# Group-weight products of a pooling branch: from one fp32 matmul to three matmuls of split operands

## The chip, the core and the metric

The kernel computes one decoder layer on one core of a Trainium2 chip. The metric is device time in microseconds (us) for one execution; less is better. Before the change it is 623.25 us, the median of three runs (622.22 to 624.1).

## What is computed

The layer takes `x` (512 tokens, 1024 channels, float32) and runs two token mixers side by side, attention and a causal pool, merges them through gates, and adds a gated MLP. The change is in the pool:

```python
proj = h @ w_in                      # q | k | v | p | gate logits
for g, w in enumerate((2, 4, 8, 16)):            # four groups of 128 channels of p
    pooled = (causal trailing mean of p over w tokens)
    diff = pooled - p
y = einsum('bsgc,gcd->bsgd', diff, w_group) * scale    # per group: 512x128 times 128x128
y_pool = y @ w_branch_pool
```

So the products in question are four, one for each group: a 128x128 weight against a 128x512 difference.

## The kernel before

Nearly all products are taken in float32r with operands cut in two. A helper `split(hi, lo, src)` (lines 72 to 78) lets ACT copy `src` into `hi` (rounded to float32r, L76) and DVE subtract `hi` from `src` into `lo` (L77). A helper `mm3` (lines 249 to 255) then issues three matmuls into one accumulator: `whi*ahi` (L251), `whi*alo` (L254), `wlo*ahi` (L255). The four group products were the exception: `pool_out(j)` took one matmul of plain float32 operands (L485), and ACT copied the result to `zT`, times the scale (L486).

**Input projections.** Two of the pooling tiles (groups 3 and 2) are plain products of 8 x 3 matmuls of 512 columns (tiles named `p`). All others are taken in pairs by a Strassen-like scheme of seven products instead of eight, `seven()` (lines 293 to 319): pair 0 is pooling groups 0 and 1, pairs 1 to 4 are the query and key tiles. Each pair needs four weight tiles, named after their product: A (a plain load), X (a sum of two loads), Y (computed on DVE from A and X, L211) and D (a half-width load). Each is split into `whi` and `wlo` before use. The banks of a pair are `sai`, `sbi`, `sci`. X of pair 1 is summed on DVE (L204). For pairs 0, 2, 3 and 4, X is loaded in two steps: SP issues a plain load into `xr` (L192), and GpSimd (POOL) issues a second DMA that adds another part of the weight onto it (L194, below called the accumulate). X of pair 2 is below called X2, and so on. A product of a pair can't begin before its tile is loaded and split.

**Pooling.** `pool_sum(j)` copies a projected tile from the accumulator to a buffer `pt` (ACT, L460), and adds shifted copies of it, log2(w) times, into buffers `pw` (L465): for group 3 on DVE, for the others on POOL. `pool_dif(j)` turns the last of them into the difference, in three DVE operations (L477, L478, L480). All these buffers come from one ring, tag `tmp`, of seven (`TMP = 7`): the eighth buffer that is drawn reuses the first, and its first writer waits for the first one's last reader. In program order group 3 draws `pt3` and four `pw`, group 2 `pt2` and three, group 0 `pt0` and one, group 1 `pt1` and two.

**What sets the order.** The source is recorded in program order; a scheduler then reorders it by its own estimate of times and writes one in-order queue for each engine. An instruction that waits holds back all that stands behind it on its engine. POOL's queue holds the pooling adds, the accumulates (L194) and the attention's bias-strip loads (L387), all in one row.

After the projections come the attention scores of the first head pair (L559; banks `sc`). `first_scores()` (line 607) takes the group products of groups 0 and 1 just before them.

Of the kernel before, what the change touches and what calls it, by code (L numbers as in the profile page):

```python
# [9 lines left out]
F32R = mybir.dt.float32r  # L10
# [4 lines left out]
P = 128  # L15
S = 512
# [14 lines left out]
PAD = 16  # L31
# [4 lines left out]
TMP = 7  # L36
# [16 lines left out]
def layer_kernel(ctx: ExitStack, tc: tile.TileContext, xT, x, w_v, w_c, rel_bias, invcnt, w_group,  # L53
                 pscale, w_br, w_out, lnr, w_fi, convp, w_fo, out):
    nc = tc.nc
# [9 lines left out]
    def bank(name):  # L65
        return ps.tile([P, S], F32, tag="ps", name=name)
# [5 lines left out]
    def split(hi, lo, src, copy=None):  # L72
        if copy:
            copy(hi, src)
        else:
            state["hi"] = nc.scalar.activation(hi, src, AF.Copy)  # L76
        state["lo"] = nc.vector.tensor_tensor(lo, src, hi.bitcast(F32), op=ALU.subtract)  # L77
        return state["lo"]
# [170 lines left out]
    def mm3(out_, w, a, start, stop, pin=False, **kw):  # L249
        (wh, wl), (ah, al) = w, a  # L250
        ins = nc.tensor.matmul(out_, wh, ah, start=start, stop=False, **kw)  # L251
        if pin:
            tc.keep_in_program_order(ins)
        nc.tensor.matmul(out_, wh, al, start=False, stop=False, **kw)  # L254
        state["mm"] = nc.tensor.matmul(out_, wl, ah, start=False, stop=stop, **kw)  # L255
# [80 lines left out]
    pb = pooling.enter_context(tc.tile_pool(name="pb", bufs=1, side="right", reuse_waits="tile"))  # L336
    wg = pb.tile([P, 4, P], F32, name="wg")
# [10 lines left out]
    for i in range(WARM):  # L348
        nc.tensor.matmul(wb_, *(nc.const_aps.tensor(1.0, [P, n], mybir.dt.bfloat16) for n in (P, S)),
                         start=True, stop=True)  # L350
# [89 lines left out]
    dif = {}  # L440
# [28 lines left out]
    def pool_dif(j, *behind):  # L469
        w = POOL_WINDOWS[j]  # L470
        pt, cur = sums.pop(j)
        with ExitStack() as held:
            for ins in behind:
                held.enter_context(tc.issue_after(ins.ins))

            d, x_ = cur[:, PAD:], pt[:, PAD:]
            nc.vector.tensor_tensor(d[:, :w - 1], d[:, :w - 1], cinv[:, :w - 1], op=ALU.mult)  # L477
            nc.vector.scalar_tensor_tensor(d[:, w - 1:], d[:, w - 1:], 1.0 / w, x_[:, w - 1:], op0=ALU.mult,  # L478
                                           op1=ALU.subtract)
            nc.vector.tensor_tensor(d[:, :w - 1], d[:, :w - 1], x_[:, :w - 1], op=ALU.subtract)  # L480
            dif[j] = d

    def pool_out(j):
        b = bank(f"zb{j}")
        nc.tensor.matmul(b, wg[:, j, :], dif[j], start=True, stop=True)  # L485
        nc.scalar.activation(zT[:, j, :], b, AF.Copy, scale=psc[:, j:j + 1])  # L486

    def in_tile(kind, j):
# [118 lines left out]
    def first_scores():  # L607
        nonlocal aw, standing
        pool_out(0)
        pool_out(1)  # L610
        pooling.close()
        aw = attn.enter_context(tc.tile_pool(name="aw", bufs=4, side="right", reuse_waits="tile"))
        standing = scores(0, True)
        next(standing)

    aw = standing = None
    for n in range(1 + pairs):
        if n == 0:
            u, done = xr[1][:, 3, :], lambda ba, u: pool_sum(0, ba)
        else:  # L620
            u = raw_k[n - 1] = qraw[n - 1][:, S:]
            done = lambda ba, u, p=n - 1: heads_done(p, ba)
        seven(("i", n), (xT_hi, xT_lo), ti, own(n), u, done, first_scores if n == 3 else None, begun.get(n))
        if n == 0:
            behind_sum.close()
            pool_dif(PLAIN[0], state["Y"])
            pool_sum(PLAIN[1], second)
            with tc.issue_after(state["acc"].ins):
                write_table(table)
        elif n == 1:  # L630
            pool_out(PLAIN[0])
            pool_dif(PLAIN[1], state["add"])
            pool_dif(0, state["add"])
            pool_sum(1, xr[1][:, 3, :], -1.0)
            add1 = state["add"]
        elif n == 2:
            pool_out(PLAIN[1])
            pool_dif(1, add1)
            with tc.issue_after(state["acc"].ins):
                load_strip(0)  # L640
                load_strip(1)
            split_heads(0, state["add"], state["copy"])
        elif n == 3:
            begin(pairs)
            list(standing)
            split_heads(1)
# [45 lines left out]
    def br_mm(f, br, b=None, ks=range(4), pin=False):  # L692
        key, o = (("br", f), 4 * br) if f >= 6 else (("oz"[br], f // 2), f % 2 * 4)
        wh, wl = split3(weights(at[key]), KT)
        b = b or bank(f"br{f}_{br}")
        for k in ks:
            src = (zT_hi[:, k, :], zT_lo[:, k, :]) if br else (oT_hi[:, k, :], oT_lo[:, k, :])
            mm3(b, (wh[:, o + k, :], wl[:, o + k, :]), src, k == 0, k == 3, pin and k == ks[0])
        return b
# [97 lines left out]
    for n, (f, br) in enumerate(order):  # L797
# [4 lines left out]
        b = br_mm(f, br)  # L802
# [17 lines left out]
    def gate_done(f, ba, u):  # L820
        if f < KT - 1:
            for br, v, scale in ((0, ba, 1.0), (1, u, -1.0)):
                nc.scalar.activation(v, v, AF.Sigmoid, scale=scale)
                nc.vector.tensor_tensor(branch[f, br], branch[f, br], v, op=ALU.mult)
            merged(f, branch[f, 0], branch[f, 1])
            unused.append(branch[f, 1])
        else:
            for br, v, scale in ((0, ba, 1.0), (1, u, -1.0)):
                gslot[8 * br + f] = unused.pop(0)
                nc.scalar.activation(gslot[8 * br + f], v, AF.Sigmoid, scale=scale)  # L830
# [6 lines left out]
    for f in range(GSEVEN, KT):  # L837
        if f == KT - 1:
# [3 lines left out]
              lambda ba, u, f=f: gate_done(f, ba, u), first_half if f == KT - 1 else None)  # L842
# [443 lines left out]
```

## Time and profile before

| | |
|---|---|
| median of three runs | 623.25 us (622.22 to 624.1) |
| the profiled execution's own time | 622.81 us |
| its span in the trace | 621.1 us |
| TensorE (PE) busy | 612.5 us, 99% of the span |
| VectorE (DVE) busy | 511.3 us, 82% |
| ScalarE (ACT) busy | 355.8 us, 57% |
| GpSimd (POOL) busy | 115.6 us, 19% |
| group products (L485) | 4 products in 8 records, from 49.8 to 73.5 us |

The trace is one execution. A row of the timeline gives start and duration in us, the engine, the line of the kernel, the operation, and out<-in by the program's tile names without their buffer numbers; a bracket at the end gives idle time ahead of it and what ended that. Matmuls are pipelined, so the start of one to the start of the next is what it costs PE, not its duration. A float32 matmul shows as two records.

### The profile page before, as it was taken

The page shows a single profiled execution, that of the slowest core. Times are in us where ns is not written, and L with a number is a line of the kernel's source. Part 1 is how long each engine was busy: PE and PEld are TensorE (multiplying, and loading weights), DVE is VectorE, ACT ScalarE, POOL GpSimd, SP SyncE. Part 2 cuts the span into 40 slices and gives each one's busy share as a digit, 9 for nine tenths or more (in the row PEclk, how much of TensorE's full clock was granted, in tenths as well). Part 3 has the DMA queues.
Part 4 walks back from the last instruction along what each step waited for, and adds up shares of the span by engine and source line. Part 5 has one row for each costly group of instructions (what it writes and reads, how often), then busy time and mean ns, then how long its engine had stood idle before and what let it go on. Part 6 is the DMA issues. An engine that isn't in the chain of part 4 may idle for free.

```text
span 621.1 us, 10681 instructions
## 1 busy us (share of the span) xinstructions
PE 612.5 (99%) x4129; PEld 553.1 (89%) x4129; DVE 511.3 (82%) x793; ACT 355.8 (57%) x541; POOL 115.6 (19%) x133
## 2 busy tenths in 40 slices
PE   9999999999999999999999999999999999999995
PEld 6899998777899998889999999999999888888884
DVE  5888876868778888399999888898988869798886
ACT  6736668557556567134676565666666355555452
POOL 0033207351212101110120010101100302123301
PEclk9999999999999999999999999999999999999998
DMA  8567544029966324807685567677635997889805
GB/s 319 196 204 199 173 147 125 35 77 298 216 173 181 75 96 143 335 5 252 128 245 124 148 180 194 182 195 202 194 84 166 330 250 146 205 189 200 209 1 135
DMA packets 41042, 107.98 MB, mean 174 GB/s; under 512 B 4240, under 2 KB 4760, under 8 KB 40736
## 3 DMA queue, kind: packets, MB, share of 16 engines
q1 hardware_dynamic: 26944, 70.72, 32.9%
q0 software_dynamic: 13472, 35.67, 29.2%
q10 hardware_dynamic: 576, 0.92, 0.4%
q8 instruction: 32, 0.52, 0.3%
q14 instruction: 18, 0.15, 0.1%
HBM read 105.18 MB, written 3.17 MB: 174 GB/s over the span
## 4 chain that ended last, share of the span: by engine, by line
PE 98%; DVE 1%; DMA 1%; DVEq 0%; issue 0%
PE saf L251 5%; PE saf L255 5%; PE saf L254 5%; PE v L435 3%; PE fi L251 3%; PE fi L255 3%; PE fi L254 3%; PE sbf L251 3%; PE sbf L254 3%; PE sbf L255 3%; PE br L251 2%; PE br L255 2%; PE br L254 2%; PE wo L251 2%; PE wo L255 2%; PE wo L254 2%
## 5 line engine op out<-in xcount | busy, mean ns | idle before, releaser
L77 DVE TENSOR_TENSOR wlo<-araw,whi 128x1024 fp32r<-128x1024 f32 x58 | 71.9, 1247 | 9.8 <-ACT whi L76 9.2
L76 ACT ACTIVATE whi<-araw 128x1024 fp32r<-128x1024 f32 x58 | 60.8, 1058 | 30.0 <-PE saf L254 6.2
L77 DVE TENSOR_TENSOR wlo<-wraw,whi 128x1024 fp32r<-128x1024 f32 (+1 forms) x47 | 55.8, 1195 | 14.9 <-ACT whi L76 14.6
L76 ACT ACTIVATE whi<-wraw 128x1024 fp32r<-128x1024 f32 (+1 forms) x47 | 47.4, 1019 | 30.2 <-DMA wraw<-in_w_fo 8.4
L76 ACT ACTIVATE whi<-tw 128x1024 fp32r<-128x1024 f32 (+1 forms) x30 | 29.5, 984 | 23.6 <-DMA tw<-in_w_fo 9.1
L77 DVE TENSOR_TENSOR wlo<-tw,whi 128x1024 fp32r<-128x1024 f32 (+1 forms) x30 | 33.5, 1130 | 6.7 <-ACT whi L76 6.7
L251 PE MATMUL saf<-hT_hi,whi 128*128 128x256 f32 x136 | 37.9, 279 | 0.0
L251 PE MATMUL sbf<-T_hi,whi 128*128 128x256 f32 x136 | 37.9, 279 | 0.0
L251 PE MATMUL saf<-nT_hi,whi 128*128 128x256 f32 x136 | 37.8, 278 | 0.0
L254 PE MATMUL saf<-hT_lo,whi 128*128 128x256 f32 x136 | 37.8, 278 | 0.0
L255 PE MATMUL saf<-nT_hi,wlo 128*128 128x256 f32 x136 | 37.8, 278 | 0.0
L254 PE MATMUL sbf<-T_lo,whi 128*128 128x256 f32 x136 | 37.7, 278 | 0.0
L255 PE MATMUL sbf<-T_hi,wlo 128*128 128x256 f32 x136 | 37.7, 278 | 0.0
L254 PE MATMUL saf<-nT_lo,whi 128*128 128x256 f32 x136 | 37.7, 277 | 0.0
L255 PE MATMUL saf<-hT_hi,wlo 128*128 128x256 f32 x136 | 37.7, 278 | 0.0
L194 POOL DMA_DIRECT2D xraw<-in_w_fi x13 | 15.7, 1205 | 116.2 <-DMA xraw<-in_w_fi 62.7
L254 PE MATMUL fi<-hT_lo,whi 128*128 128x256 f32 (+1 forms) x112 | 36.2, 326 | 0.0
L255 PE MATMUL fi<-hT_hi,wlo 128*128 128x256 f32 (+1 forms) x112 | 36.2, 326 | 0.0
L251 PE MATMUL fi<-hT_hi,whi 128*128 128x256 f32 (+1 forms) x112 | 36.1, 327 | 0.0
L239 POOL DMA_DIRECT2D tw<-in_w_fo x18 | 15.6, 902 | 59.8 <-DVE wlo L77 59.8
L595 POOL TENSOR_SCALAR pp<-pp,rs 128x128 f32<-128x128 f32 (+3 forms) x32 | 21.1, 680 | 25.0 <-DVE rs L592 25.0
L254 PEld LDWEIGHTS saf<-hT_lo,whi 128*128 128x128 f32 x136 | 25.5, 188 | 0.0
(359 smaller groups left out, 2208.9 us busy)
## 6 DMA issues: line engine op xcount, KB each, us to landing
tw<-in_w_fo POOLq DMA_DIRECT2D x20, 512.0 KB, 7.4
araw<-in_w_fi SPq DMA_DIRECT2D x17, 512.0 KB, 3.8
xraw<-in_w_fi SPq DMA_DIRECT2D x13, 512.0 KB, 3.9
xraw<-in_w_fi POOLq DMA_DIRECT2D x13, 512.0 KB, 6.6
araw<-in_w_c SPq DMA_DIRECT2D x12, 512.0 KB, 4.6
wraw<-in_w_fi SPq DMA_DIRECT2D x10, 512.0 KB, 3.7
wraw<-in_w_fo SPq DMA_DIRECT2D x10, 512.0 KB, 5.5
tw<-in_w_fo SPq DMA_DIRECT2D x10, 512.0 KB, 6.9
```

The costliest lines, as they stand in the source:

```text
L76: state["hi"] = nc.scalar.activation(hi, src, AF.Copy)
L77: state["lo"] = nc.vector.tensor_tensor(lo, src, hi.bitcast(F32), op=ALU.subtract)
L194: state["acc"] = nc.gpsimd.dma_start(v, bass.AP(tensor=a.tensor, offset=a.offset, ap=[[pst, pn], [u.offset + S - a.offset, 2], [est, S]]), ...
L239: nc.gpsimd.dma_start(raw, half(then[1:], sl), accum_op=ALU.add)
L251: ins = nc.tensor.matmul(out_, wh, ah, start=start, stop=False, **kw)
L254: nc.tensor.matmul(out_, wh, al, start=False, stop=False, **kw)
L255: state["mm"] = nc.tensor.matmul(out_, wl, ah, start=False, stop=stop, **kw)
L435: ins = nc.tensor.matmul(bs[j], xs_[j][a], (wh, wl)[b], start=kt == 0 and n == 0, stop=False)
L595: state["norm"] = nc.gpsimd.tensor_scalar(pp[:, offs[i]:offs[i] + n], pp[:, offs[i]:offs[i] + n], rs[:, i:i + 1], 1.0, op0=ALU.mult, op1=A ...
```

## The change

The group weight `wg` is split once, when the first difference is formed. Each difference is split into two new buffers, `hi` and `lo`, which are drawn from the same ring of seven as the sums. The product becomes `mm3`.

```diff
@@ pool_dif / pool_out
-            dif[j] = d
+            if not dif:
+                split(*wgs, wg)
+            dif[j] = tuple(pb.tile([P, PAD + S], F32R, tag="tmp", name=f"dif{j}_{q}", bufs=TMP)[:, PAD:]
+                           for q in ("hi", "lo"))
+            split(*dif[j], d)
+
+    wgs = [pb.tile([P, 4, P], F32R, name=f"wg_{q}") for q in ("hi", "lo")]
 
     def pool_out(j):
         b = bank(f"zb{j}")
-        nc.tensor.matmul(b, wg[:, j, :], dif[j], start=True, stop=True)
+        mm3(b, tuple(w[:, j, :] for w in wgs), dif[j], True, True)
         nc.scalar.activation(zT[:, j, :], b, AF.Copy, scale=psc[:, j:j + 1])
```

In program order `pool_sum(2)` stands behind `pool_dif(3)`, so `pt2`, which was the sixth buffer of the ring, is now the eighth and reuses `pt3`. The split of `wg` stands early on ACT, ahead of the splits of the pairs' operands. From the first group product to the scores the scheduler writes other queues; behind the first scores the queues stand as they did.

POOL's queue from group 2's sum to the first strip load, before. The names behind "waits" are semaphores: `DMAHW7` tells of the plain load of X2, `DMAHW2` of X3's, `DMAHW5` of X4's.

```order
L459 MEMSET pt_523 128x16
L465 TENSOR_TENSOR pw_1_526<-pt_523 128x527 [waits Activation_49,Pool_49]
L465 TENSOR_TENSOR pw_2_528<-pw_1_526 128x525 [waits DVE_49,Pool_49]
L465 TENSOR_TENSOR pw_4_530<-pw_2_528 128x521 [waits DVE_49,Pool_49]
L194 DMA xr_106<-in_w_c 128x2x512 [waits DMAHW7_49,DVE_49]
L459 MEMSET pt_582 128x16
L194 DMA xr_106<-in_w_c 128x2x512 [waits DMAHW2_49,DVE_49]
L465 TENSOR_TENSOR pw_1_585<-pt_582 128x527 [waits Activation_49,Pool_49]
L459 MEMSET pt_666 128x16
L465 TENSOR_TENSOR pw_1_669<-pt_666 128x527 [waits Activation_49,Pool_49]
L465 TENSOR_TENSOR pw_2_671<-pw_1_669 128x525 [waits PE_49,Pool_49]
L194 DMA xr_106<-in_w_c 128x2x512 [waits DMAHW5_49,DVE_49]
```

The same piece after. Here are also the strip loads, ahead of group 1's sum.

```order
L459 MEMSET pt_531 128x16 [waits DVE_49]
L465 TENSOR_TENSOR pw_1_534<-pt_531 128x527 [waits DVE_49,Activation_49,Pool_49]
L465 TENSOR_TENSOR pw_2_536<-pw_1_534 128x525 [waits DVE_49,Pool_49]
L194 DMA xr_106<-in_w_c 128x2x512 [waits DMAHW2_49,DVE_49]
L465 TENSOR_TENSOR pw_4_538<-pw_2_536 128x521 [waits Pool_49]
L194 DMA xr_106<-in_w_c 128x2x512 [waits DMAHW7_49]
L459 MEMSET pt_590 128x16 [waits DVE_49]
L465 TENSOR_TENSOR pw_1_593<-pt_590 128x527 [waits PE_49,Activation_49,Pool_49]
L194 DMA xr_106<-in_w_c 128x2x512 [waits DMAHW5_49,DVE_49]
L387 DMA strip_820<-F_d 128x512 [waits DMAHW3_49,DMASW1_49]
L387 DMA strip_822<-F_d 128x512
...
L459 MEMSET pt_684 128x16 [waits DVE_49,Pool_49]
```

The accumulates of X2 and X3 have changed places, and an add stands between them; group 1's sum has moved behind X4's accumulate and the strip loads.

ACT's queue, from the split of a tile of pair 1 (`whi_472`, now `whi_474`) to the copy of group 0's tile (`pt_582`, now `pt_590`); before, with group 2's copy `pt_523`, which stood further up, as the first row:

```order
L460 ACTIVATE pt_523<-p_391 128x512
...
L76 ACTIVATE whi_472<-xr_106 128x1024
L76 ACTIVATE whi_476<-xr_107 128x512
L76 ACTIVATE whi_540<-araw_316 128x1024
L289 ACTIVATE xr_107<-sai_533 128x256
L76 ACTIVATE whi_592<-araw_468 128x1024
```

and after:

```order
L76 ACTIVATE whi_474<-xr_106 128x1024
L76 ACTIVATE whi_478<-xr_107 128x512
L76 ACTIVATE dif_hi<-pw_8_379 128x512
L289 ACTIVATE xr_107<-sai_541 128x256
L76 ACTIVATE whi_548<-araw_318 128x1024
L460 ACTIVATE pt_531<-p_393 128x512
L76 ACTIVATE whi_600<-araw_470 128x1024
```

Group 2's copy, which stood eight rows ahead of the piece's third split, now stands behind the split of group 3's difference.

PE's queue where pair 2's first X product (bank `sbi2`, weight `whi15` = X2 split) begins, before:

```order
L251 MATMUL sci2_674<-xT_hi_73,whi14_592 128x256
L254 MATMUL sci2_674<-xT_lo_74,whi14_592 128x256
L255 MATMUL sci2_674<-xT_hi_73,wlo14_593 128x256
L251 MATMUL sbi2_706<-iT3_hi_100,whi15_609 128x256
L254 MATMUL sbi2_706<-iT3_lo_101,whi15_609 128x256
```

and after:

```order
L254 MATMUL sai1_541<-inT1_lo_99,whi11_474 128x256
L255 MATMUL sai1_541<-inT1_hi_98,wlo11_475 128x256
L251 MATMUL sbi2_724<-iT3_hi_100,whi15_617 128x256
L254 MATMUL sbi2_724<-iT3_lo_101,whi15_617 128x256
L251 MATMUL sai1_541<-xT_hi_73,whi13_548 128x256
L254 MATMUL sai1_541<-xT_lo_74,whi13_548 128x256
```

It has moved behind pair 1's second X product; two of its matmuls are followed by pair 1's last Y product (`whi13`). In the changed queue 82 matmuls of 256 columns and 3 of 512 stand between the first matmul of group 3's product (whose place is that of the first L485 before) and this one; 132 of 256 columns and 6 of 512 stand between this one and the first matmul of group 1's product, which now stands directly ahead of the scores.

## Prediction

> **What bounds the kernel now.** I began with the page: its span and the chain of work that ended last. Then I asked for the busy time of each engine in the stage of the change (after the window's length: PE, weight loads, DVE, ACT, POOL, each with its instructions, then PE's granted clock and the DMA), and for the waits of PE in it, of which there are none.
>
> ```profile
> span 621.1 us, 10681 instructions
> PE 98%; DVE 1%; DMA 1%; DVEq 0%; issue 0%
> ```
>
> ```profile
> 40.00:50.00 10.00, 10.00 (x88) 10.00 (x87) 8.27 (x12) 5.73 (x9) 5.33 (x5) 1.00 0.71 184
> 50.00:60.00 10.00, 10.00 (x84) 9.52 (x83) 7.19 (x11) 5.69 (x11) 4.94 (x5) 1.00 0.74 192
> 60.00:70.00 10.00, 10.00 (x78) 9.04 (x77) 8.55 (x18) 7.31 (x12) 3.48 (x6) 1.00 0.69 181
> 70.00:80.00 10.00, 10.00 (x87) 9.14 (x86) 8.29 (x14) 5.63 (x8) 0.00 (x0) 1.00 0.41 156
> sum 40.00, PE 40.00 PEld 37.70 DVE 32.30 ACT 24.36 POOL 13.75; mean PE 10.00 PEld 9.42 DVE 8.08 ACT 6.09 POOL 3.44
> ```
>
> PE carries 98% of the chain, and in the 40 us around the group products it isn't idle once, at full clock. So two things count: what the new products cost PE, and whether anything now comes too late for PE. A wait of PE here is paid in full, as PE sets the pace to the end of the program and nothing behind gives it back. The profiled execution took 622.81 us, 0.44 less than the median of the runs; terms worked out from it are added to the median.
>
> **PE's own cost.** The page's durations of matmuls overlap, so I take distances between starts.
>
> ```profile
> 30.28 0.39 PE L251 MATMUL p<-xT_hi,whi 128*128 128x512 f32 x1
> 30.51 0.39 PE L254 MATMUL p<-xT_lo,whi 128*128 128x512 f32 x1
> ...
> 49.84 1.02 PE L485 MATMUL zb<-pw,wg 128*128 128x512 f32 x2
> 50.30 0.68 PE L251 MATMUL sai<-inT_hi,whi 128*128 128x256 f32 x1
> 50.82 0.28 PE L254 MATMUL sai<-inT_lo,whi 128*128 128x256 f32 x1
> ...
> 54.65 0.28 PE L255 MATMUL sai<-inT_hi,wlo 128*128 128x256 f32 x1
> ...
> 55.11 0.28 PE L251 MATMUL sbi<-iT_hi,whi 128*128 128x256 f32 x1
> ```
>
> A 256-column matmul costs 0.46 / 4 = 0.115 us (54.65 to 55.11), a 512-column one of split operands 0.23. From 49.84 to 50.82 stand one float32 product and one 256-column matmul, so the product costs 0.98 - 0.115 = 0.87. Three matmuls cost 3 x 0.23 = 0.69. Each product gains 0.18, all four 0.7 us. That is the whole gain that the change can bring.
>
> **The splits as work.** Five more ACT copies and five more DVE subtractions of 128x512 (the weight and four differences). Their rows, from splits of the same shape:
>
> ```profile
> 56.63 0.63 ACT L76 ACTIVATE whi<-xr 128x512 fp32r<-128x512 f32 x1 [0.71 <-ACT quad L306]
> ```
>
> ```profile
> 57.29 0.69 DVE L77 TENSOR_TENSOR wlo<-xr,whi 128x512 fp32r<-128x512 f32 x1
> ```
>
> That is 3.2 us of ACT and 3.5 us of DVE. DVE has 40 - 32.3 = 7.7 us idle in the four windows and ACT 15.6, so as work they cost nothing; the cover is that idle time. If it were gone, DVE's 3.5 us would be the price.
>
> **The queues: X2 comes late.** This is where I expect the time. POOL's rows before:
>
> ```profile
> 39.91 1.06 POOL L465 TENSOR_TENSOR pw<-pt 128x527 f32<-128x527 f32 x1 [7.13 <-DVE araw L211]
> 41.05 3.06 POOL L465 TENSOR_TENSOR pw<-pw 128x525 f32<-128x525 f32 x2
> 44.13 1.24 POOL L194 DMA_DIRECT2D xr<-in_w_c  x1
> ...
> 54.90 1.20 POOL L194 DMA_DIRECT2D xr<-in_w_c  x1 [9.40 <-DMA xr<-in_w_c]
> 55.66 1.55 POOL L465 TENSOR_TENSOR pw<-pt 128x527 f32<-128x527 f32 x1
> ```
>
> ```profile
> L465 POOL TENSOR_TENSOR pw<-pw x3: 1062/1063/1916, 41.1 to 59.0; 128x525 f32<-128x525 f32 x2, 128x521 f32<-128x521 f32 x1
> ```
>
> ```profile
> 50.31 0.38 SPq L192 DMA_DIRECT2D xr<-in_w_c  x1
> ```
>
> ```profile
> L194 POOL DMA_DIRECT2D xr<-in_w_c x3: 1203/1203/1238, 44.1 to 63.0; - x3
> ...
> DMA to landing us min/median/max: 5.9/7.1/7.6
> ```
>
> ```profile
> L192 SPq DMA_DIRECT2D xr<-in_w_c x3: 378/379/379, 39.2 to 56.1; - x3
> ...
> DMA to landing us min/median/max: 4.0/4.3/6.4
> ```
>
> Before, X2's accumulate starts at 44.13, right behind group 2's sum, and lands 7.1 later, at 51.2; PE takes X2 up at 55.11. The next accumulate, X3's, waits 9.4 us, because X3's plain load only leaves SP at 50.31 and lands 4.0 later. In the changed queue X3's accumulate stands ahead of X2's, with an add between. X2's, ready at 44, has to sit out that wait. Group 2's sum is late as well: its `pt2` now reuses `pt3`'s buffer, whose last reader ended before at about 47.1 (below), and its copy stands on ACT behind the split of group 3's difference. I put the two adds that still stand ahead between 50.5 and 53.5, so the load decides.
>
> ```profile
> 43.12 1.54 DVE L204 TENSOR_TENSOR xr<-xr,xr 128x512 f32<-128x512 f32 x1
> ...
> 46.39 0.68 DVE L204 TENSOR_TENSOR xr<-xr,araw 128x512 f32<-128x512 f32 x1
> 46.99 0.16 DVE L480 TENSOR_TENSOR pw<-pw,pt 128x15 f32<-128x15 f32 x1
> ```
>
> X3's plain load follows a DVE split of X1, which shares its home. DVE gets 0.69 more work ahead of it (`wg_lo`), but loses the company of POOL's adds, beside which one operation took 1.54 us and its twin 0.68 without. I take 50.0 for its issue (49.7 to 51.0). Then: landing at 54.0; POOL starts 0.6 later (54.90 against 50.31 + 4.0), at 54.6; the next instruction 0.76 behind (55.66 less 54.90), at 55.4; the add 1.06 to 1.92, I take 1.5, between an add alone and one beside DVE; X2's accumulate at 57.0; its landing 5.9 to 7.6, I take 6.6, since it runs beside X3's accumulate but behind its first 2.4 us; that is 63.6. The split's copy on ACT:
>
> ```profile
> 53.58 1.06 ACT L76 ACTIVATE whi<-xr 128x1024 fp32r<-128x1024 f32 x1 [0.89 <-PE sai L254]
> ```
>
> With 0.1 for the signal, `whi15` is there at 64.75. PE gets to its first X2 matmul after 82 x 0.115 + 3 x 0.23 = 10.1 us from 49.84, at 60.0. It waits **4.7 us** (3.2 with every early end, 7.7 with every late one).
>
> The Trainium skill, "SBUF — State Buffer", section "Who interferes with whom", says that a DVE instruction with two SBUF inputs and a GpSimd one that reads SBUF shut each other out, the later for the earlier one's whole length. The rows of 1.54 and 1.92 us agree with that; by it the add between the accumulates could cost 1.06 plus a whole DVE split (1.22, row below), an estimate of 2.3, and the sum would be 0.8 us higher.
>
> **What queues up behind X2.** Three smaller waits follow.
>
> ```profile
> 53.52 0.69 DVE L211 TENSOR_TENSOR araw<-xr,araw 128x512 f32<-128x512 f32 x1
> ...
> 54.86 1.22 DVE L77 TENSOR_TENSOR wlo<-xr,whi 128x1024 fp32r<-128x1024 f32 x1
> ...
> 59.93 0.42 DVE L312 TENSOR_TENSOR quad<-quad,sai 128x256 f32<-128x256 f32 x1 [1.95 <-PE sai L255]
> 60.38 0.43 DVE L313 TENSOR_TENSOR sai<-xr,sci 128x256 f32<-128x256 f32 x1
> ```
>
> DVE stands at the sum for pair 2's Y (L211), which needs X2 too. Behind it are the second L211 and pair 1's L312 and L313, which read and write the bank that PE wants two matmuls after X2: with overlaps of some 0.08 each about 2.0 us from X2's landing. PE is there at 1.16 + 0.23 = 1.4. It waits **0.6** (0.4 to 0.8). ACT has a row of splits behind `whi15`: one of 512 columns, three of 1024, two 512 copies, then pair 2's L303, without which the D product can't go on in its bank:
>
> ```profile
> 61.78 0.39 ACT L303 ACTIVATE quad<-sbi 128x256 f32<-128x256 f32 x1
> ```
>
> With `whi15` itself, and at 0.1 us overlap each, that is 0.06 + 4 x 0.96 + 3 x 0.53 + 0.39 = 5.9 us from the landing; PE, with 24 matmuls behind the last wait, is there at 2.0 + 2.8 = 4.8. It waits **1.1** (0.5 to 1.5). Last, group 1's sum on POOL stands behind X4's accumulate and four strip loads, and PE needs both halves of its difference directly ahead of the scores. From X2's landing: 2.4 for its splits (1.06 and 1.22, with 0.1 for a signal), 4.3 to 6.4 for X4's plain load, 0.6 and 0.8 for its accumulate, 2.2 for the strips,
>
> ```profile
> 63.78 2.68 POOL L387 DMA_DIRECT2D strip<-F_d  x4
> ```
>
> 3.1 for two adds (1.55 and 1.06) and, an estimate, 0.5 for clearing the pad, and 2.2 to 4 for the difference and its split among DVE's other splits: 15.6 to 19.5. PE, with 132 x 0.115 + 6 x 0.23 = 16.6 and the waits above of 1.7, is there 1.2 + 18.3 = 19.5 after it. By that it just fits. The splits from DVE's queue there can add to it, and I put **0.5** (0 to 1.5).
>
> The sum: 4.7 + 0.6 + 1.1 + 0.5 - 0.7 = 6.2 us. From the median that is 623.25 + 6.2 = **629.4 us**; the profiled execution would show 629.0. Early ends give 3.2 + 0.4 + 0.5 - 0.7 = 3.4 (626.6), late ones 7.7 + 0.8 + 1.5 + 1.5 - 0.7 = 10.8 (634.0); all late at once is unlikely.
>
> **The rivals.** *X2 still in time* (the other side: not slower). If X2 landed by 58.8, PE would find it split at 60.0, the three later waits would go too, and only the 0.7 us of PE would be left: 622.5. For that X2's accumulate must start by 52.2. For it speaks the slack before, landing at 51.2 and used at 55.11. Against it: it stands behind an accumulate whose load leaves at about 50. Chance 0.08.
>
> *DVE's work alone.* If POOL's order costs little but the cover of DVE is not where its new work falls, 3.5 us come on the path, most of all in 60 to 70 us, where DVE is busy 8.55 of 10: 3.5 - 0.7, 626.0 us. It decides where a new subtraction is the last thing that a matmul waits for. Against it speaks that PE's order puts other work between a split's first and last use. Chance 0.10.
>
> *The clock falls in the wait.* The end of the trace shows what idle time does:
>
> ```profile
> 613.41 0.28 PE L255 MATMUL foa<-whi,sd_lo 128*128 128x256 f32 x1
> ```
>
> ```profile
> 615.00:618.00 3.00, 0.00 (x0) 0.00 (x0) 2.86 (x9) 0.00 (x0) 0.00 (x0) 0.95 0.64 236
> 618.00:621.10 3.10, 0.00 (x0) 0.00 (x0) 0.32 (x1) 0.00 (x0) 0.00 (x0) 0.50 0.31 104
> ```
>
> The last matmul ends at 613.7; the granted clock is 0.5 in the last window and 0.95 over the one before, so it halved at 618 - 0.3 = 617.7, after 4.0 us of idleness. A wait of 4.7 us is just past that. No row shows how long the clock stays down; if as long as it took to fall, 4 us at half clock lose 2.0 us, less what PE would have waited anyway (1.1 and 0.5): 0.4 to 2.0, middle 1.2, 630.6 us. Chance 0.20. The Trainium skill, "TensorE: Matmul & The Clock Gate", section "Part 1: The HAM clock gate (the "warmup" mystery)", has the clock halve after an idle window of about 3.4 us that runs freely, and come back after a busy one. The 4.0 us agree; by it a wait of 4.7 us meets a whole window about four times in ten, and 3.4 us at half clock would lose 1.7, an estimate.
>
> **How the numbers follow.** The forecast, late X2 at full clock, gets 0.60, the clock 0.20, DVE alone 0.10, X2 in time 0.08, and 0.02 is left for faster than I can account for. The measurement tells 0.3% from no change, 1.9 us here: 621.4 and 625.1 are the bounds. X2 in time lies within them; so does the lowest end of DVE alone, 0.01. Slower is 0.60 + 0.20 + 0.09 = 0.89, same 0.09, faster 0.02. The range goes from DVE alone, with half a us to spare, 625.5, to 633.5, which holds all but the last of the late ends and of the clock; outside are X2 in time and those ends.
>
> **What would show it.** Right: in POOL's rows X3's accumulate ahead of X2's, X2's at about 57; a PE wait of 4 to 5 us between 59 and 66 whose releaser is ACT's `whi<-xr` (L76); short PE waits on DVE L313 and ACT L303 within 6 us behind it; one at the last `zb`, on DVE; PE busy elsewhere; three `zb` matmuls 0.23 apart. Wrong: PE busy throughout 50 to 80 us, X2's accumulate landing before 59, or waits of PE whose releaser is a split of a difference and not of X2.

## The result, and the profile after

The changed kernel takes 629.71 us, the median of four runs (629.56 to 630.3), against 623.54 us for the kernel before on the same chip (four runs, 622.22 to 624.1). The ratio is 1.0111, with a 95% interval of 1.0096 to 1.0127: slower by about 6.9 us (6.0 to 7.9 by the interval). The two medians are 6.2 us apart; the differences below go by the ratio. The profiled execution took 630.3 us.

From the page of the changed kernel, the span, PE's granted clock in forty slices, and the chain of work that ended last:

```profile
span 628.6 us, 10688 instructions
...
PEclk9999899999999999999999999999999999999998
...
PE 94%; DVE 2%; DMA 2%; POOL 1%; issue 0%; ACT 0%; DVEq 0%; SPq 0%; POOLq 0%
```

PE had 98% of the chain before and has 94% now. Apart from the last slice, where the matmuls are over, one shows a lower clock: the fifth, 63 to 79 us. The waits of PE from 40 to 90 us, of which there were none before (after the colon: us in total, number, longest):

```profile
PE sbi L251 <- ACT whi L76: 3.8, 1, 3.8
PE zb L254 <- DVE dif_lo L77: 0.5, 1, 0.5
PE sbi L251 <- ACT quad L303: 0.5, 1, 0.5
PE sai L251 <- DVE sai L313: 0.2, 1, 0.2
```

These are the four places that the prediction named. The long one is the wait for X2's split. POOL's rows ahead of it, in the order of its queue (group 2's first two adds, X3's accumulate, the third add, X2's accumulate):

```profile
49.95 1.50 POOL L465 TENSOR_TENSOR pw<-pt 128x527 f32<-128x527 f32 x1 [15.09 <-DVE wlo L77]
51.52 1.92 POOL L465 TENSOR_TENSOR pw<-pw 128x525 f32<-128x525 f32 x1
53.41 1.24 POOL L194 DMA_DIRECT2D xr<-in_w_c  x1
54.26 1.49 POOL L465 TENSOR_TENSOR pw<-pw 128x521 f32<-128x521 f32 x1
55.40 1.51 POOL L194 DMA_DIRECT2D xr<-in_w_c  x1
```

X2's accumulate starts at 55.4; it started at 44.1 before. On PE the last row ahead of the wait, the first X2 product, and the row behind which ACT's and DVE's queues are caught up; then the last group product and the first score:

```profile
59.23 0.28 PE L255 MATMUL sai<-inT_hi,wlo 128*128 128x256 f32 x1
63.36 0.58 PE L251 MATMUL sbi<-iT_hi,whi 128*128 128x256 f32 x1 [3.85 <-ACT whi L76]
...
68.77 0.38 PE L255 MATMUL sbi<-iT_hi,wlo 128*128 128x256 f32 x1
68.98 0.28 PE L251 MATMUL sbi<-iT_hi,whi 128*128 128x256 f32 x1
69.10 0.28 PE L254 MATMUL sbi<-iT_lo,whi 128*128 128x256 f32 x1
...
83.78 0.40 PE L251 MATMUL zb<-dif_hi,wg_hi 128*128 128x512 f32 x1
84.67 0.50 PE L254 MATMUL zb<-dif_lo,wg_hi 128*128 128x512 f32 x1 [0.49 <-DVE dif_lo L77]
...
85.34 0.39 PE L565 MATMUL sc<-kh,ql 64*128 64x256 f32 x2
```

From 68.77 to 68.98 a matmul of 256 columns costs 0.21 us, from 68.98 to 69.10 again 0.12. The cause is the granted clock, which the busy time by stretches shows (us, then PE's busy time and records; the granted clock is the third number from the right):

```profile
55.33:58.74 3.41, 3.41 (x32) 3.41 (x31) 0.42 (x1) 0.77 (x2) 2.76 (x4) 1.00 0.95 154
58.74:62.15 3.41, 0.77 (x7) 0.57 (x5) 0.00 (x0) 0.00 (x0) 0.00 (x0) 1.00 0.87 155
62.15:65.56 3.41, 2.02 (x7) 1.73 (x8) 3.24 (x7) 3.08 (x4) 0.00 (x0) 0.50 0.02 5
65.56:68.97 3.41, 3.41 (x17) 3.41 (x17) 3.41 (x7) 2.38 (x4) 0.00 (x0) 0.50 0.55 186
```

The clock halved at 62.15, 2.8 us after PE had gone idle, and stayed down for 6.8 us. In the kernel before the first score is at

```profile
78.16 0.39 PE L559 MATMUL sc<-kh,ql 64*128 64x256 f32 x2
```

So from the first group product (49.84 before, 49.17 now) to the first score it was 28.3 us and is 36.2: 7.85 more. Behind the first score the stages are as long as they were (542.9 us to the end of the span before, 543.3 now). The parts of the 7.85: 4.0 at X2 (63.36 less 59.35, when PE was free), 0.4 at L313, 0.6 at L303, 0.8 at the last product, 2.3 by the clock (the 23 matmuls that start in the two stretches, 0.213 less 0.115 each), less 0.7 for PE's cheaper products. That is 7.4. Most of the 0.45 left lies straight behind two of the waits: the matmuls at 63.36 and 64.34 took 0.38 us each to the next start, where the others at half clock took 0.21, so 0.34 in all.

### The profile page after: what moved, and what is told of

Same layout as the page of the kernel before. It is cut to its first block, busy times and chain, and to the rows that moved or that the text cites. A ratio compares the mean times of both kernels' runs of the same rounds, so it can differ in the third digit from the quotient of the medians.

```text
span 628.6 us, 10688 instructions
## 1 busy us (share of the span) xinstructions
PE 615.0 (98%) x4133; PEld 555.5 (88%) x4133; DVE 512.7 (82%) x798; ACT 358.3 (57%) x546; POOL 116.7 (19%) x133
## 4 chain that ended last, share of the span: by engine, by line
PE 94%; DVE 2%; DMA 2%; POOL 1%; issue 0%; ACT 0%; DVEq 0%; SPq 0%; POOLq 0%
PE saf L251 5%; PE saf L254 5%; PE saf L255 5%; PE v L435 3%; PE fi L251 3%; PE fi L255 3%; PE fi L254 3%; PE sbf L251 3%; PE sbf L255 2%; PE sbf L254 2%; PE br L251 2%; PE br L255 2%; PE br L254 2%; PE wo L255 2%; PE wo L251 2%; PE wo L254 2%
## 5 line engine op out<-in xcount | busy, mean ns | idle before, releaser
L254 PE MATMUL fi<-hT_lo,whi 128*128 128x256 f32 (+1 forms) x112 | 36.2, 326 | 0.0
L255 PE MATMUL fi<-hT_hi,wlo 128*128 128x256 f32 (+1 forms) x112 | 36.2, 326 | 0.0
L251 PEld LDWEIGHTS saf<-hT_hi,whi 128*128 128x128 f32 x136 | 25.5, 188 | 0.0
```

## The experiments

The theory after the result: X2 is late by its place in POOL's queue; all else follows from it. Three questions were open: what puts X2's accumulate there, whether the new splits cost something by themselves, and what the clock adds. All times against the kernel before on the same chip; the difference is the ratio times that kernel's median.

| run | median us | before | ratio, 95% interval | difference us |
|---|---|---|---|---|
| the change | 629.71 | 623.54 | 1.0111 (1.0096 to 1.0127) | +6.9 |
| nine buffers | 629.56 | 622.21 | 1.0115 (1.0101 to 1.0129) | +7.2 |
| X3's accumulate behind X2's | 629.64 | 622.21 | 1.0109 (1.0090 to 1.0128) | +6.8 |
| both | 628.46 | 622.21 | 1.0104 (1.0088 to 1.0120) | +6.5 |
| kernel before, accumulates exchanged | 629.53 | 622.21 | 1.0123 (1.0105 to 1.0141) | +7.7 |
| group 2's copy first | 625.87 | 622.23 | 1.0056 (1.0043 to 1.0069) | +3.5 |
| and group 1's adds first | 624.93 | 622.23 | 1.0045 (1.0032 to 1.0057) | +2.8 |
| X2 not held | 626.54 | 622.23 | 1.0067 (1.0054 to 1.0081) | +4.2 |
| thirty matmuls in the wait | 628.07 | 622.23 | 1.0101 (1.0072 to 1.0130) | +6.3 |
| both copies first | 622.76 | 622.30 | 1.0002 (0.9993 to 1.0010) | +0.1 |
| the same, no subtractions | 621.51 | 622.30 | 0.9987 (0.9978 to 0.9995) | -0.8 |
| the same, subtractions on POOL | 622.94 | 622.30 | 1.0007 (0.9999 to 1.0016) | +0.4 |
| thirty-eight matmuls in the wait | 628.90 | 622.30 | 1.0102 (1.0087 to 1.0117) | +6.3 |

**Nine buffers in the ring.**

```diff
-TMP = 7
+TMP = 9
```

> The changed kernel with nine buffers in the ring `tmp` in place of seven; POOL's order stays: X3's accumulate, one add of group 2's sum, X2's accumulate. Theory (queue): what holds X2 is X3's accumulate, which waits for X3's plain load until about 53.4; so X2's accumulate stays at about 55.4, PE's wait at about 3.8 us, and the time at 629.7 us, at most 0.5 less. Rival (ring): X2 is late because group 2's sum waits for a buffer of the ring; with nine buffers that sum would be done by 45, the wait of PE would go, and the time would be 622.5 to 623.5. Rival (split work): the buffers alone change little, 629 to 630, but then with waits on splits of differences.

Measured: 629.56, no change. PE's wait for X2 is 3.6 us, and the other three waits are the same to 0.1. Group 2's copy on ACT runs at 49.06, as late as in the changed kernel (49.21), where the last reader of `pt3`'s buffer had ended at 45.96. The ring is not the cause.

**X3's accumulate behind X2's.** In `fetch_raw`:

```diff
+            with ExitStack() as behind_acc:
+                if key == ("i", 3):
+                    behind_acc.enter_context(tc.issue_after(state["acc"].ins))
-            state["acc"] = nc.gpsimd.dma_start(
+                state["acc"] = nc.gpsimd.dma_start(
...
```

> The changed kernel with X3's accumulate put behind X2's in POOL's queue; the ring still has seven buffers. Theory (queue): X2's accumulate now stands behind group 2's adds alone, which end at about 53.4 in the changed kernel; it starts at 53.4 instead of 55.4, lands at about 60.0, `whi` is there at 61.2 and PE, which arrives at 59.3, waits 1.9 us; that is under the 2.9 us after which the clock fell, so full clock throughout: 629.7 - 1.9 - 2.7 = 625.1, range 624 to 627. Rival (ring): the ring's late sum is what counts, so PE's wait falls by under 0.5 us and the time stays over 628.5. Rival (split work): 629 to 630.

Measured: 629.64, no change either; the expected 625.1 was wrong. POOL's rows of this run, from group 2's first add to X2's accumulate:

```profile
49.97 3.78 POOL L468 TENSOR_TENSOR pw<-pt 128x527 f32<-128x527 f32 x1 [15.27 <-DVE wlo L77]
53.82 2.19 POOL L468 TENSOR_TENSOR pw<-pw 128x525 f32<-128x525 f32 x2
55.96 1.23 POOL L197 DMA_DIRECT2D xr<-in_w_c  x1
```

X2's accumulate now waits for the adds alone, and they are as late as X3's load was: 55.96 against 55.40. The first add took 3.78 us here, beside DVE's splits, and 1.50 in the changed kernel, where the two DVE splits beside it took 4.10 us instead of 2.35. PE waits 3.1 and 1.1 us, both times for splits on ACT, and the clock falls as well.

**Both of these.**

> Both together: nine buffers and X3's accumulate behind X2's. Theory (queue): X2's accumulate starts at about 44 as before the change, lands at about 51, and PE has no wait for X2; the follow-up waits go as well, the clock stays up, and what is left is PE's gain of 0.7 us, less up to 0.7 at the last group product, whose sum still stands behind the strip loads: 622.5 to 623.5 us against 623.5 for the kernel before. Rival (split work): the subtractions and copies cost up to 2.8 us net whatever the queue: 625.5 to 626.5.

Measured: 628.46, 6.5 above the kernel before where 0 was expected. So with a free buffer and X2 ahead of X3 the loss is still there, and the theory as it stood fell. The rows that show why are ACT's: the split of group 3's difference, and group 2's copy (`pt<-p`).

```profile
49.54 0.61 ACT L76 ACTIVATE dif_hi<-pw 128x512 fp32r<-128x512 f32 x1
50.07 0.39 ACT L292 ACTIVATE xr<-sai 128x256 f32<-128x256 f32 x1
50.35 1.05 ACT L76 ACTIVATE whi<-araw 128x1024 fp32r<-128x1024 f32 x1
51.30 0.59 ACT L463 ACTIVATE pt<-p 128x512 f32<-128x512 f32 x1
```

The copy runs as soon as ACT gets to it; no wait is shown ahead of it. It stands there because the queue has it behind `dif_hi`. POOL's first add starts 0.15 us after the copy's end here (52.04 after 51.89), in the changed kernel (49.95 after 49.80) and in the kernel before (39.91 after 39.76), so it is the copy that it waits for, although the row of the changed kernel names a split on DVE that ended at about the same time. In the kernel before the same copy ran more than ten us earlier:

```profile
39.16 0.60 ACT L460 ACTIVATE pt<-p 128x512 f32<-128x512 f32 x1 [2.06 <-PE p L255]
```

The new theory: the late copy makes group 2's sum late, and X2's accumulate, which the code queues behind that sum (line 146), with it. X3's load is a second hold of about the same length, beside the first: in the changed kernel it landed at 52.8 (49.02 and 3.8), and group 2's second add ended at 53.4, just as X3's accumulate began. So taking away either one alone gains nothing.

**The accumulates exchanged in the kernel before.** No split, one fp32 product per group; only X2's accumulate is issued behind X3's.

```diff
+            def accumulate():
-            state["acc"] = nc.gpsimd.dma_start(
+                state["acc"] = nc.gpsimd.dma_start(
...
+            if key == ("i", 2):
+                state["held"] = accumulate
+            else:
+                accumulate()
+                if key == ("i", 3):
+                    with tc.issue_after(state["acc"].ins):
+                        state["held"]()
```

> The kernel before, with its one float32 product per group and no split, and only X2's accumulate moved behind X3's in POOL's queue. Theory (queue): X3's accumulate starts at about 54.9 as before, X2's at about 55.7, it lands at about 62.3, `whi` is there at 63.4; PE arrives at 60.0 and waits 3.4 us (2.5 to 4.5), with 0.5 to 2 us of follow-up waits and up to 2.7 us if the clock falls: 627 to 630.5 us. Rival (split work or the products themselves): without them nothing is lost: 623 to 624.

Measured: 629.53, within the range. PE's waits in it:

```profile
PE sbi L260 <- ACT whi L76: 3.8, 1, 3.8
PE sbi L264 <- DVE wlo L77: 0.8, 1, 0.8
```

The whole loss comes without any of the new work. A late X2 is enough.

**Group 2's copy first.** The two calls change places in the code.

```diff
-            pool_dif(PLAIN[0], state["Y"])
+            y0 = state["Y"]
             pool_sum(PLAIN[1], second)
+            pool_dif(PLAIN[0], y0)
```

> The changed kernel with two calls exchanged in the code: group 2's sum is written ahead of group 3's difference, so that ACT's queue has group 2's copy (`pt`, L460) ahead of the split `dif_hi` again; seven buffers, all splits, all twelve matmuls. Theory (late copy): the copy runs at about 39 instead of 49, group 2's adds end at about 44, X2's accumulate starts behind them at about 44, and PE waits neither for X2 nor behind it; the clock stays up. What is left is PE's 0.7 us less, with up to 0.7 back at the last group product: the time of the kernel before, or up to 0.7 us under it. Rival (contention): the new splits on DVE beside POOL's adds still cost 2 us or more: over 1.5 us above the kernel before. Rival (load): X3's plain load alone holds X2: no change, 6 to 7 us above the kernel before.

Measured: 625.87; half of the loss is gone. The copy, X2's accumulate behind the adds, and all waits of PE up to 130 us:

```profile
38.26 0.60 ACT L460 ACTIVATE pt<-p 128x512 f32<-128x512 f32 x1 [1.79 <-PE p L255]
```

```profile
43.36 1.24 POOL L194 DMA_DIRECT2D xr<-in_w_c  x1
```

```profile
PE zb L254 <- DVE dif_lo L77: 1.1, 1, 1.1
PE zb L251 <- ACT dif_hi L76: 0.6, 1, 0.6
PE sbi L255 <- DVE wlo L77: 0.4, 1, 0.4
```

The wait for X2 is gone, as the theory has it; the time was to be that of the kernel before, and is not. A new wait stands at the last difference, and the clock fell once more behind it.

**And group 1's adds first.** Beside that, X4's accumulate is queued behind group 1's sum, as X2's is behind group 2's.

```diff
-                    if (n, f, q) == ("i", 2, "X"):
+                    if (n, f, q) in (("i", 2, "X"), ("i", 4, "X")):
```

> As the run before, and in POOL's queue group 1's sum stands ahead of X4's accumulate and of the strip loads, as in the kernel before. Theory (late copy): the wait at the last group product goes as well (0.5 us in the changed kernel), so PE has no wait between 40 and 95 us and the time is 0.5 to 0.9 us under the kernel before. Rival (contention): over 1.5 us above it.

Measured: 624.93, again above what was expected. Group 1's copy on ACT, then POOL's adds and X4's accumulate behind them:

```profile
69.20 0.62 ACT L460 ACTIVATE pt<-xr 128x512 f32<-128x512 f32 x1
```

```profile
69.95 4.06 POOL L465 TENSOR_TENSOR pw<-pt 128x527 f32<-128x527 f32 x1 [5.29 <-ACT pt L460]
74.10 1.06 POOL L465 TENSOR_TENSOR pw<-pw 128x525 f32<-128x525 f32 x1
75.10 1.20 POOL L194 DMA_DIRECT2D xr<-in_w_c  x1
```

Before, these adds ran at 57.3 and 59.0 and the accumulate at 63.0. It is the same thing a second time: group 1's copy, too, stands behind a split of a difference (`dif_hi`, 67.22). Of the 12 us by which the accumulate is late, 2.5 are the first add's own: it took 4.06 us, 1.57 before, with two DVE splits running beside it (70.74 to 73.1). X4 is now late, and PE waits 1.2 us for L313 behind it.

**X2 not held.** The copy stays late; the line that queues X2's loads behind the sum is taken out.

```diff
-                    if (n, f, q) == ("i", 2, "X"):
-                        held.enter_context(tc.issue_after(state["sum"].ins))
```

> The changed kernel without the line that queues X2's loads behind group 2's sum; ACT's copy stays late and the sum with it. Theory (late copy): the copy hurts only by way of X2's accumulate; that now starts as soon as X2's plain load has landed, at about 43.5, so PE does not wait for X2; group 2's product, whose sum is still late, may bring a wait of up to 1 us: from 0.7 us under the kernel before to 1 us above it. Rival: the late sum itself, or the splits, cost the time, and not X2: 4 to 7 us above the kernel before.

Measured: 626.54, 4.2 above the kernel before, at the lower edge of what the rival gave. X2's accumulate starts at 43.78, and PE does not wait for X2; but it waits 0.9 and 1.1 us for the last difference and 0.8 for a split on DVE. The theory's 1 us was too little: with X2 free 2.7 of the 6.9 us are gone, and what is left stands for the most part at the last difference, as in the run with group 2's copy first, and the clock fell there too (at 81.12).

**Both copies first.** Group 2's calls exchanged as above, nine buffers, and:

```diff
+            pool_sum(1, xr[1][:, 3, :], -1.0)
             pool_dif(PLAIN[1], state["add"])
             pool_dif(0, state["add"])
-            pool_sum(1, xr[1][:, 3, :], -1.0)
```

> The changed kernel with both sums of the groups (group 2's and group 1's) written ahead of the differences that stood before them, and nine buffers in the ring, so that ACT has both copies (`pt`, L460) and POOL its adds and accumulates in the order of the kernel before. All splits, all twelve matmuls. Theory (late copies): in the run with one copy moved and group 1's adds ahead of X4's accumulate, that accumulate started at 75.1 (63.0 before), because group 1's copy was late; this costs 1.4 us at pair 2's close, 0.7 at the last difference, 0.3 at an earlier group's output; with the copy early these go. Left are 0.7 us at the first product, where X1's split on DVE comes behind the weight's, against 0.7 gained on PE: within 0.5 us of the kernel before. Rival (split work): the five subtractions cost it wherever the copies stand: 2 to 3 us above the kernel before, as in the run before.

Measured: 622.76, a ratio of 1.0002. Group 2's copy and group 1's on ACT are early again:

```profile
38.93 0.60 ACT L460 ACTIVATE pt<-p 128x512 f32<-128x512 f32 x1 [1.79 <-PE p L255]
```

```profile
55.56 0.63 ACT L460 ACTIVATE pt<-xr 128x512 f32<-128x512 f32 x1
```

One wait of PE is left between 20 and 130 us:

```profile
PE sbi L255 <- DVE wlo L77: 0.4, 1, 0.4
```

With all splits and all twelve matmuls in place, 6.9 us became 0.1 (interval -0.4 to 0.6): the loss came from where the two sums, with their copies, stood in the queues.

**The same without the subtractions.** The lo tiles are no longer drawn:

```diff
-            split(*dif[j], d)
+            nc.scalar.activation(dif[j][0], d, AF.Copy)
...
-    wgs = [pb.tile([P, 4, P], F32R, name=f"wg_{q}") for q in ("hi", "lo")]
+    wgs = [pb.tile([P, 4, P], F32R, name="wg_hi")] * 2
```

> As the run with both copies moved, but the five subtractions of the new splits (the weight's and the four differences') are left out, and the products take the high parts in the place of the low ones; five copies on ACT and twelve matmuls stay. It prices DVE's part of the split work. Theory (late copies): about 0.7 us under the kernel before, since the one wait that is left (at the first product) came from the weight's subtraction; 0.5 to 1.0 us under the run with both copies moved. Rival (split work): if that run stays 2 to 3 us above the kernel before, this one goes to 0 to 0.7 under it. If both are alike, the subtractions cost nothing.

Measured: 621.51, 0.8 us under the kernel before (interval 0.3 to 1.4). Here PE's gain of 0.7 us is seen in the time. The five subtractions take it back: 0.9 us between the two ratios.

**The subtractions on POOL.**

```diff
-            split(*dif[j], d)
+            nc.scalar.activation(dif[j][0], d, AF.Copy)
+            nc.gpsimd.tensor_tensor(dif[j][1], d, dif[j][0].bitcast(F32), op=ALU.subtract)
```

and the same for `wg`.

> As the run with both copies moved, but the five subtractions are made on POOL and not on DVE; results as in the changed kernel. Theory (late copies): POOL is idle from 45 to 54, where group 3's falls, and the weight's falls ahead of 31, so X1's split is in time again and PE waits at most 0.5 us in all: 0.2 to 0.7 us under the kernel before. Rival (POOL's queue): X3's or X4's accumulate, each behind a subtraction of 1.1 to 2 us that waits for DVE and ACT, comes late and PE waits 1 us or more: 0.5 us or more above the kernel before.

Measured: 622.94, 0.4 us above the kernel before, with an interval that reaches down to no change. The view of waits names none for PE, yet the expected gain isn't there. Between first product and first score this run took 28.5 us, both copies first 28.4, the run without subtractions 27.7. PE's rows show where the 0.8 us against the run without subtractions lie, in gaps too short for the view: 0.4 at the matmul with X1's `wlo` behind the first product's start (0.72 us from 49.50 to 50.22, where the two matmuls alone take 0.35), 0.2 behind that product's end, and 0.3 at a later product's `dif_lo` (69.51). The first has a likely cause in DVE's row of X1's two splits: 2.92 us from 48.72, beside POOL's subtraction for group 3 (49.02 to 51.1), where the run without subtractions has 1.82. No run tests that, and the other two stay open.

**Thirty matmuls in the wait.** Ahead of X2's first matmul, on constants and into the bank that it clears:

```diff
+            if key == ("i", 2):
+                for n in range(WAIT_MM):
+                    with tc.issue_after(state["mm"].ins):
+                        state["mm"] = nc.tensor.matmul(low, ..., start=True, stop=True)
```

> The changed kernel with thirty matmuls of 256 columns on constants ahead of X2's first one, into the bank that X2 clears: about 3.4 us in which PE only passes the time. X2 stays as late as it is. Theory (clock counts): PE is then not idle for longer than 1 us, the granted clock stays at 1.0 through 40 to 95 us, and of the 2.7 us that the matmuls at half clock cost, 2.0 to 2.7 are saved: 627.0 to 627.7 us, 4 to 5 above the kernel before. Rival (covered): PE would have waited that time anyway behind X2 (for ACT's copies and the last difference), so the time stays within 0.5 us of the changed kernel, 6 to 7 above the kernel before.

Measured: 628.07, with single runs from 626.94 to 631.37: unclear by its time. The trace says more. The clock stayed up at 62 us, where it had fallen, but fell one stretch later:

```profile
58.84:62.26 3.42, 3.42 (x32) 3.09 (x31) 0.24 (x1) 0.31 (x1) 0.00 (x0) 1.00 0.71 129
62.26:65.67 3.41, 1.91 (x14) 1.40 (x13) 3.38 (x6) 3.28 (x4) 0.00 (x0) 1.00 0.00 0
65.67:69.08 3.41, 3.41 (x19) 3.41 (x18) 3.41 (x7) 0.39 (x1) 0.00 (x0) 0.50 0.70 227
```

In the middle stretch PE's idle times are two, of 0.4 and 1.1 us, far below the 4.0 us that the prediction took for the limit.

**Thirty-eight.**

```diff
-WAIT_MM = 30
+WAIT_MM = 38
```

> The changed kernel with thirty-eight matmuls on constants ahead of X2's first one (thirty in the earlier run). The granted clock changed in all runs on a grid of 3.41 us: it halved behind a stretch in which PE was busy 0.5 to 1.9 us, and stayed behind one with 2.25. With thirty, the stretch from 62.3 to 65.7 had 1.9. Theory (busy share): eight more make it 2.4, the clock stays at 1.0 up to the end of the scores, and the 11 matmuls that the stretch at half clock lost are back: 1.3 us less than with thirty, 4.3 to 5.0 us above the kernel before; the delay of 0.5 us to X2's first two matmuls is lost in the wait of 1.1 us that follows. Rival (idle time): the clock goes by how long PE is idle at a time, not by its share; then it had no reason to fall with thirty either, and the eight change nothing or add 0.5 us.

Measured: 628.90; no gain. On the clock the first theory was right:

```profile
61.93:65.34 3.41, 2.93 (x25) 2.51 (x23) 3.13 (x5) 3.21 (x4) 0.00 (x0) 1.00 0.00 0
```

The clock stayed at 1.0 to the end of the program's matmuls. On the time it was wrong: PE, faster now, waits 0.6 us for a DVE split, 0.5 for ACT's and 0.3 for the last difference. From the first product to the last score this run takes 79.4 us, the changed kernel 81.0; so of the 2.3 us lost at half clock at most 1.6 are net in these two profiles, and between the ratios it is 0.6, within their intervals. How much of the loss is the clock's is settled no better than that.

## Why the prediction was right, point by point

**The number.** 629.4 was forecast, 629.71 measured. The mechanism is the forecast one; that the number is so close is partly luck, as its sizes cancel. The waits are 5.8 us where the likeliest case had 6.9, and the clock, which that case left out, adds up to 2.3 that PE's other waits cover in part.

**PE's own cost**, 0.18 us per product: right. In the run without subtractions the three matmuls of the first product start at 49.63, 49.86 and 50.09, 0.23 us apart, and its time shows 0.8 (0.3 to 1.4) for all four. In the changed kernel the prediction's sign, three `zb` matmuls 0.23 apart, did not show: other matmuls stand between the first one (49.17) and the other two (52.18 and 52.42).

**The splits cost nothing as work**: wrong, by a size that the loss hides. With the queues in order the five subtractions cost about 0.9 us, most of it at the first product (with both copies first 1.11 us from 49.69 to 50.80, where the two matmuls alone take 0.23 and 0.115), where X1's split on DVE comes behind the weight's. DVE's idle time of 7.7 us in the four windows did not cover that, since it lay elsewhere: from the weight's split at 45.03 to X1's at 49.32 DVE had none. And the five copies on ACT, which as work cost nothing, are what the loss begins with: those of the differences stand ahead of the copies of the sums.

**X2 late behind X3's accumulate**: right, and the kernel before with the exchange alone shows it. The steps: X3's plain load issued at 49.0 (50.0 forecast), its accumulate at 53.4 (54.6), the add 1.49 us (1.5), X2's accumulate at 55.4 (57.0), the landing 6.8 us later (6.6), the wait 4.0 us (4.7; 3.2 to 7.7). Of the 1.6 us by which X2's accumulate came earlier, 0.7 are the profiled run's earlier start, 0.3 the load's issue, 0.2 its quicker landing (3.8 us), and 0.4 that the accumulate began 1.14 us after the add did and not at its end. The add's price by the Trainium skill ("SBUF — State Buffer", "Who interferes with whom") would have been 2.3, an estimate; here it took 1.49. That the two engines hold each other up, the traces confirm, and either may pay: the changed kernel's earlier adds took 1.5 and 1.9 us and the two DVE splits beside them 4.10 instead of 2.35; with X3 behind X2 an add took 3.78 and the splits 2.35.

**"So the load decides"**: the step that failed as an explanation. The prediction saw the second hold (group 2's sum, 50.5 to 53.5) and set it aside as the shorter. It is as long: without the load X2's accumulate starts at 55.96. And the reason given for the late sum, that `pt2` now reuses `pt3`'s buffer, is not what held it: with nine buffers nothing changes. What the prediction put second, that the copy "stands on ACT behind the split of group 3's difference", is the cause: with the two calls exchanged the copy runs at 38.26 and the wait for X2 is gone. The prediction had the right row and weighed it as a side remark.

**The smaller waits**: 0.4 at L313 (0.6 forecast), 0.6 at L303 (1.1), 0.8 at the last product (0.5). Each within its range. For the last one the prediction named the strip loads. In the changed kernel two holds ran side by side here too: the pad was cleared behind the strips by 73.4, and group 1's copy, behind the differences' splits, ended at 73.7. The sum was done at 76.5, but DVE took up the difference only at 80.1: pair 2's L312, which waited 2.5 us for PE, and four more instructions stand ahead of it in DVE's queue. So no single cause is shown for the wait of the changed kernel. With X2 in time and the strips put behind the adds it was the copy that held them; with the copy early as well the wait is gone.

**The rival of the clock**, given 0.20, came true beside the forecast and not against it. Its limit was mis-sized: 4.0 us idle, from the end of the trace, where 2.8 us were enough. The time at half clock was 6.8 us instead of 4, the loss up to 2.3 instead of 0.4 to 2.0.

**The other rivals.** X2 in time, 622.5, did not happen, and would not have given that number: with X2 in time 3.5 us of loss remain (group 2's copy first). DVE's work alone, 2.8 us above the kernel before, was not the path either: with both copies first the subtractions cost 0.9, and what remained with group 2's copy first came from group 1's.

## What to carry to other kernels

When a change adds an instruction to an engine that "has time", look at what stands behind it in that engine's queue before pricing its work: a copy of 0.6 us that slides ten us back can hold a transfer on another queue, and that transfer the engine that sets the pace. If two holds of like length run side by side, taking away one shows nothing, so test them together and one by one. Here the mended order costs two moved calls and nine buffers, and gives the kernel before back (1.0002), no more: the 0.7 us won on PE go to the five subtractions.

## What the runs showed of the hardware

The granted clock changed only on a grid of 3.41 us. In the changed kernel it fell at 62.15 and at 625.35: 165 steps of 3.413. What went with it was how much PE had done in the stretch that ended there, not one long idle time. With PE busy for 0.0, 0.5, 0.6, 0.8, 0.8, 1.0, 1.5, 1.65 or 1.9 us of 3.41 the next stretch ran at half clock; with 2.25 or 2.9 it did not. The busy time of these views gives no sharp limit, though: at the end of the program, stretches with 1.75 us (group 2's copy first) and 1.84 (the accumulates exchanged), each with over 1.5 us idle in one piece, were followed by one more at full clock. What exactly is counted stays open. At half clock, stretches with 1.45, 2.0, 2.3 and 2.6 us were followed by another at half clock, those with 2.95 and more by full clock. The run with group 2's copy first has a case in which two short waits, 0.6 and 1.1 us, were enough:

```profile
75.70:79.11 3.41, 1.65 (x12) 1.14 (x10) 3.41 (x7) 1.42 (x3) 0.00 (x0) 1.00 0.02 5
79.11:82.52 3.41, 3.41 (x20) 2.51 (x20) 1.48 (x7) 0.69 (x1) 0.00 (x0) 0.50 0.00 0
```

and in the run after it a stretch behind which the clock stayed:

```profile
82.11:85.52 3.41, 2.25 (x18) 1.85 (x16) 3.38 (x12) 2.94 (x5) 0.00 (x0) 1.00 0.25 100
85.52:88.93 3.41, 3.18 (x23) 2.64 (x24) 3.41 (x8) 1.62 (x4) 0.00 (x0) 1.00 0.08 12
```

The Trainium skill, "TensorE: Matmul & The Clock Gate", section "Part 1: The HAM clock gate (the "warmup" mystery)", has a free-running window of 3413 ns; the grid agrees. It speaks of an idle window; here a window that was more than half busy (1.9 of 3.41 us) sufficed, and the measurement decides. Such a stretch costs less than it seems: at half clock PE comes later to the waits behind it, and the run that kept the clock up gained between 0.6 and 1.6 us of the 2.3.
